# Sums and differences of the up-projection's operands formed on GpSimd instead of VectorE

## The chip, the cores and the metric

The kernel runs on one core of one Trainium2 chip. The metric is device time of one execution in microseconds. A core has five engines with an instruction queue each: TensorE (PE, matmuls), VectorE (DVE), ScalarE (ACT), GpSimd (POOL) and SyncE (SP, which issues most DMAs). Each queue is worked off in order; an instruction that waits holds up everything behind it in its queue. Matmuls read their operands from SBUF and write PSUM.

## The reference

One decoder block over 2048 positions of 1024 channels, in float32:

```
h = rms_norm(x, norm1_g);  z = h @ w_in
y_mix = concat(rg_lru(conv(lru_x)) * gelu(lru_gate),  sc_b * conv(sc_c * sc_x))
x = x + y_mix @ w_out
h = rms_norm(x, norm2_g)
gate, up = split(causal_dwconv(h @ w_up, ffn_conv_w))      # 2 * 3072 columns
x = x + (gelu(gate) * up) @ w_down
return rms_norm(x, final_g)
```

The part that matters is `h @ w_up`: h is 1024 channels by 2048 positions, w_up 1024 by 6144.

## The kernel before

Activations lie with channels on the 128 partitions and positions along the columns. The 2048 positions are handled in two halves of 1024, each half as two blocks of 512 (t0 and t1). Every float32 product is made of three matmuls: each operand is split into a rounded high part and the remainder, the low part, and high x high, high x low and low x high are added. The split (`split`, L196) is one ACT instruction (L197, high) and one DVE instruction (L198, low = source - high).

The three large products (w_out, w_up, w_down) use Strassen's scheme in Winograd's form: seven products of blocks instead of eight, at the price of sums and differences of blocks. For the up-projection the activation's 2 x 2 blocks are a[t0], a[t1] (channels of the upper half) and b[t0], b[t1] (channels of the lower half). `h_prep(half, k, rs)` makes all operands of channel tile k, one of four per half: it loads a and b from DRAM, scales both with the norm (L564), and forms T1 = a0 - a1, T2 = -T1 - b1, T3 = b1 - a1 and T4 = -T2 - b0, of 128 x 512 each. T1 and T2 go into tile hc, T3 over a's second block, T4 into hq. Then a (with T3), b and c are split at 128 x 1024 (hhB/hlB twice, hhT/hlT), and T4 at 128 x 512 (ht).

The program runs through: in-projection and mixers of half 0 and w_out's product ("o"), the same for half 1, up-projection of half 0, w_down's product ("d") of half 0, up-projection of half 1, w_down's product of half 1. A w_out or w_down product is a function `sweeps`: seven sweeps, one for each block product, of three (o) or six (d) steps. A step reads one weight page and one activation page by DMA, splits both (wh/wl and fh/fl), and runs 24 matmuls; the page buffers hold two and a half steps, so the high part of the next-but-one step's activation can be split only when PE is done with a step. Tile names carry sweep and step: fl_o_1_1 is the low part of the activation of sweep 1, step 1 of "o". After a sweep, DVE adds the four PSUM tiles into the results (L785).

The calls of `h_prep` lie beside these products: for half 0 one near the end of half 1's in-projection and three in half 1's "o" product (after its steps 3, 8 and 14, counted from 0); for half 1 four in half 0's "d" product (after steps 4, 12, 25 and 34). Groups are counted from 0 within each half below. The results are used in the up-projection that follows.

The order on PE, SP and GpSimd is that of the program text. ACT and DVE are ordered by a scheduler, from priorities (splits of sweep pages are moved ahead by HW = 90 places) and its own estimate of when inputs are ready. GpSimd has little work: it clears and copies the two or three columns that the convolutions carry from one half to the other (L285, L287, L292), and issues DMAs that add weights (L365).

Of the kernel before, what the change touches and what calls it, by code (L numbers as in the profile page):

```python
# [9 lines left out]
AF = mybir.ActivationFunctionType  # L10
ALU = mybir.AluOpType
# [57 lines left out]
def block_kernel(  # L69
# [11 lines left out]
    nc = tc.nc  # L81
# [35 lines left out]
    def col(o):  # L117
        return g1[:, o : o + 1] if o < KC else prm[:, o - KC : o - KC + 1]
# [4 lines left out]
    def act(name):  # L123
        return page(name, "act", 28)
# [4 lines left out]
    def tmp(name):  # L129
        return page(name, "tmp", 7)  # L130

    def big(name, side):
        return ub.tile([P, T + 3], F32, name=name, tag="ab"[side], bufs=2)
# [10 lines left out]
    def flat(t):  # L144
        return t.rearrange("p a b -> p (a b)")

    def r32(ap):
        return ap.bitcast(F32R)

    def blk(b):  # L150
        return slice(b * NB, (b + 1) * NB)
# [44 lines left out]
    def split(hi, lo, src):  # L196
        nc.scalar.activation(r32(hi), src, AF.Copy)  # L197
        nc.vector.tensor_tensor(r32(lo), src, hi, ALU.subtract)  # L198
# [360 lines left out]
    def h_prep(half, k, rs):  # L559
        a = big(f"ha{half}_{k}", 0)[:, :T]  # L560
        b = big(f"hb{half}_{k}", 0)[:, :T]
        for t, kk in ((a, k), (b, k + 4)):
            nc.sync.dma_start(t, x2_d[half][kk // 2][kk % 2])
            nc.vector.scalar_tensor_tensor(t, t, col(O_G2 + kk), rs, ALU.mult, ALU.mult)  # L564
        c = flat(tmp(f"hc{half}_{k}"))
        q = flat(tmp(f"hq{half}_{k}"))[:, :NB]
        t0, t1 = blk(0), blk(1)
        nc.vector.tensor_tensor(c[:, t0], a[:, t0], a[:, t1], ALU.subtract)
        nc.vector.scalar_tensor_tensor(c[:, t1], c[:, t0], -1.0, b[:, t1], ALU.mult, ALU.subtract)
        nc.vector.tensor_tensor(a[:, t1], b[:, t1], a[:, t1], ALU.subtract)  # L570
        nc.vector.scalar_tensor_tensor(q, c[:, t1], -1.0, b[:, t0], ALU.mult, ALU.subtract)
        out = {}
        for t, names in ((a, ("B11", "T3")), (b, ("B21", "B22")), (c, ("T1", "T2"))):
            hi, lo = act(f"hh{names[0]}{half}_{k}"), act(f"hl{names[0]}{half}_{k}")
            split(flat(hi), flat(lo), t)
            for i, n in enumerate(names):
                out[n] = (hi[:, i, :], lo[:, i, :])
        t4 = act(f"ht{half}_{k}")
        split(t4[:, 0, :], t4[:, 1, :], q)
        out["T4"] = (t4[:, 0, :], t4[:, 1, :])  # L580
        return out

# [281 lines left out]
    def beside_mixers(n):  # L864
        mean0(n)
        if n == NOUT - 2:
            hs[0].append(h_prep(0, 0, rs2[0][0]))
# [10 lines left out]
    def h_beside(half, at):  # L878
        def beside(s):
            if s in at:  # L880
                hs[half].append(h_prep(half, len(hs[half]), rs2[half][0]))

        return beside
# [172 lines left out]
```

## Time and profile before

| What | us |
|---|---|
| median of 3 runs | 2283.89 (2283.12 to 2284.76) |
| the profiled execution's own time | 2283.66 |
| its span, first to last instruction | 2281.9 |
| PE (matmul) busy | 2265.3 (99%) |
| DVE busy | 1723.0 (76%) |
| ACT busy | 1133.6 (50%) |
| POOL busy | 153.3 (7%) |
| mean granted TensorE clock | 0.998 of full speed |

Rows of a timeline read: start, duration (us), engine, line, operation, output<-inputs, shape, count, and in brackets the idle time of the engine before it and what ended it. Rows of groups read: line, engine, operation, tiles, shape, count, busy us, mean ns of one, idle before. Rows of waits read: who waited for whom, then us in total, times, longest. Buffer numbers are left out of names there: fl_o stands for all low parts of "o". A stretch's row (windows) reads: us, then busy us (instruction count) of PE, PEld (TensorE's weight loads), DVE, ACT and POOL, granted clock, share of DMA time, GB/s.

### The profile page before, as it was taken

The page shows a single profiled execution, that of the slowest core. Times are in us where ns is not written, and L with a number is a line of the kernel's source. Part 1 is how long each engine was busy: PE and PEld are TensorE (multiplying, and loading weights), DVE is VectorE, ACT ScalarE, POOL GpSimd, SP SyncE. Part 2 cuts the span into 40 slices and gives each one's busy share as a digit, 9 for nine tenths or more (in the row PEclk, how much of TensorE's full clock was granted, in tenths as well). Part 3 has the DMA queues.
Part 4 walks back from the last instruction along what each step waited for, and adds up shares of the span by engine and source line. Part 5 has one row for each costly group of instructions (what it writes and reads, how often), then busy time and mean ns, then how long its engine had stood idle before and what let it go on. Part 6 is the DMA issues. An engine that isn't in the chain of part 4 may idle for free.

```text
span 2281.9 us, 26199 instructions
## 1 busy us (share of the span) xinstructions
PE 2265.3 (99%) x9982; PEld 1873.6 (82%) x9982; DVE 1723.0 (76%) x1912; ACT 1133.6 (50%) x1247; POOL 153.3 (7%) x232
## 2 busy tenths in 40 slices
PE   9999999999999999999999999999999999999997
PEld 7888888888888878888888888888888888888886
DVE  8765668767657798888888887587888888876556
ACT  6554625554557255544444454354544444444343
POOL 0010000011100000111111100000100000000000
PEclk9999999999999999999999999999999999999999
DMA  7553248778654586233232357676223232359755
GB/s 260 147 125 103 70 162 290 266 195 216 185 135 138 180 280 216 76 104 114 93 115 93 116 188 268 216 243 209 70 97 116 93 116 93 116 182 321 259 193 175
DMA packets 146447, 378.30 MB, mean 166 GB/s; under 512 B 14160, under 2 KB 17872, under 8 KB 145744
## 3 DMA queue, kind: packets, MB, share of 16 engines
q1 hardware_dynamic: 136384, 357.74, 45.4%
q0 software_dynamic: 9792, 18.88, 5.3%
q8 instruction: 78, 1.28, 0.2%
q14 instruction: 49, 0.40, 0.1%
q10 hardware_dynamic: 144, 0.00, 0.0%
HBM read 289.53 MB, written 124.78 MB: 182 GB/s over the span
## 4 chain that ended last, share of the span: by engine, by line
PE 98%; DVE 1%; DMA 0%; issue 0%; ACT 0%; SPq 0%; DVEq 0%
PE zin_b L240 27%; PE zx L628 23%; PE dx L748 11%; PE zc L628 11%; PE dy L748 9%; PE za L628 6%; PE ox L748 6%; PE oy L748 4%; PE zr_b L240 1%; PE zi_b L240 1%; DVE x2r L929 0%; DMA x<-in_xT 0%; DVE fl_o L198 0%; PE ms_b L272 0%; PE ms_a L272 0%
## 5 line engine op out<-in xcount | busy, mean ns | idle before, releaser
L240 PE MATMUL zin_b<-xh,wh_in 128*128 128x512 f32 x896 | 276.2, 389 | 1.0 <-ACT xh L413 0.6
L240 PE MATMUL zin_b<-xl,wh_in 128*128 128x512 f32 x896 | 276.1, 389 | 0.1
L240 PE MATMUL zin_b<-xh,wl_in 128*128 128x512 f32 x896 | 275.9, 389 | 0.0
L240 PEld LDWEIGHTS zin_b<-xh,wh_in 128*128 128x128 f32 x896 | 168.2, 188 | 36.5 <-ACT xh L413 0.9
L240 PEld LDWEIGHTS zin_b<-xl,wh_in 128*128 128x128 f32 x896 | 168.2, 188 | 35.3 <-DVE xl L414 0.5
L240 PEld LDWEIGHTS zin_b<-xh,wl_in 128*128 128x128 f32 x896 | 168.2, 188 | 34.9
L198 DVE TENSOR_TENSOR fl_d<-wrf_d,fh_d 128x1024 fp32r<-128x1024 f32 x84 | 102.8, 1224 | 119.6 <-ACT fh_d L197 117.2
L197 ACT ACTIVATE fh_d<-wrf_d 128x1024 fp32r<-128x1024 f32 x84 | 89.0, 1060 | 201.8 <-PE dx L748 84.3
L198 DVE TENSOR_TENSOR wla_up<-wra_up,wha_up 128x1024 fp32r<-128x1024 f32 x48 | 58.8, 1226 | 140.7 <-ACT wha_up L197 140.6
L748 PE MATMUL dx<-fh_d,wh_d 128*128 128x512 f32 x384 | 149.4, 389 | 0.0
L748 PE MATMUL dx<-fl_d,wh_d 128*128 128x512 f32 x384 | 149.4, 389 | 0.0
L748 PE MATMUL dx<-fh_d,wl_d 128*128 128x512 f32 x384 | 149.4, 389 | 0.0
L628 PE MATMUL zc<-hhB,whd_up 128*128 128x512 f32 x384 | 126.0, 389 | 0.0
L301 DVE SCALAR_TENSOR_TENSOR cu<-un,prm,cu 128x1024 f32<-128x1024 f32 x96 | 122.6, 1277 | 4.3 <-ACT cu L297 4.3
L301 DVE SCALAR_TENSOR_TENSOR cg<-ug,prm,cg 128x1024 f32<-128x1024 f32 x96 | 122.7, 1278 | 0.4
L639 ACT ACTIVATE ug<-zx 128x512 f32<-128x512 f32 x96 | 57.6, 600 | 126.0 <-PE zx L628 126.0
L197 ACT ACTIVATE wh_in<-wr_in 128x1024 fp32r<-128x1024 f32 x53 | 55.7, 1055 | 129.1 <-PE zin_b L240 87.4
L628 PE MATMUL zx<-ht,whc_up 128*128 128x512 f32 x384 | 118.2, 389 | 0.0
L198 DVE TENSOR_TENSOR wl_d<-wrw_d,wh_d 128x1024 fp32r<-128x1024 f32 x84 | 102.4, 1219 | 12.7 <-ACT wh_d L197 11.4
L748 PE MATMUL dy<-fh_d,wh_d 128*128 128x512 f32 x288 | 112.0, 389 | 0.0
L748 PE MATMUL dy<-fl_d,wh_d 128*128 128x512 f32 x288 | 112.0, 389 | 0.0
L748 PE MATMUL dy<-fh_d,wl_d 128*128 128x512 f32 x288 | 112.0, 389 | 0.0
(265 smaller groups left out, 5556.6 us busy)
## 6 DMA issues: line engine op xcount, KB each, us to landing
wr_in<-in_w_in SPq DMA_DIRECT2D x53, 512.0 KB, 6.8
wra_up<-in_w_up SPq DMA_DIRECT2D x48, 512.0 KB, 4.6
wrb_up<-in_w_up SPq DMA_DIRECT2D x48, 512.0 KB, 5.2
f_d_T<-cg SPq DMA_DIRECT2D x96, 256.0 KB, 2.5
wrw_d<-sd_d_S SPq DMA_DIRECT2D x48, 512.0 KB, 4.5
wrf_d<-f_d_T SPq DMA_DIRECT2D x48, 512.0 KB, 3.9
f_d_B<-cu SPq DMA_DIRECT2D x72, 256.0 KB, 2.4
wrw_d<-in_w_down SPq DMA_DIRECT2D x36, 512.0 KB, 4.6
```

What stands on the lines that cost most here:

```text
L197: nc.scalar.activation(r32(hi), src, AF.Copy)
L198: nc.vector.tensor_tensor(r32(lo), src, hi, ALU.subtract)
L240: nc.tensor.matmul(ps[t], r32(a), r32(b[:, blk(t)]), start=(first and i == 0), stop=(last and i == 2))
L301: nc.vector.scalar_tensor_tensor(dst, src[:, k : k + T], col(o_w + k), dst, ALU.mult, ALU.add)
L628: nc.tensor.matmul(ps, r32(p[:, s]), r32(self.hs[k][x][o]), start=f and i == 0, stop=l and i == 2, skip_group_check=True,)
L639: nc.scalar.activation(dst, self.x, AF.Copy)
L748: nc.tensor.matmul(ps[m], r32(p), r32(x[:, k, :]), start=first and i == 0 and n == 0, stop=(last or not on_x) and i == ni - 1 and n == 2, ...
```

## The change

In `h_prep` the four sums and differences move from DVE to GpSimd. GpSimd forms them with plain additions and subtractions, so five are needed: q = a1 - a0, T1 = a0 - a1, T2 = q - b1, T3 = b1 - a1, and q = T2 + b0, which is -T4. The sign of T4 is put right in its split: ACT copies q with scale -1, and DVE forms -q - high in one instruction. All other lines are the same.

```diff
-        nc.vector.tensor_tensor(c[:, t0], a[:, t0], a[:, t1], ALU.subtract)
-        nc.vector.scalar_tensor_tensor(c[:, t1], c[:, t0], -1.0, b[:, t1], ALU.mult, ALU.subtract)
-        nc.vector.tensor_tensor(a[:, t1], b[:, t1], a[:, t1], ALU.subtract)
-        nc.vector.scalar_tensor_tensor(q, c[:, t1], -1.0, b[:, t0], ALU.mult, ALU.subtract)
+        nc.gpsimd.tensor_tensor(q, a[:, t1], a[:, t0], ALU.subtract)
+        nc.gpsimd.tensor_tensor(c[:, t0], a[:, t0], a[:, t1], ALU.subtract)
+        nc.gpsimd.tensor_tensor(c[:, t1], q, b[:, t1], ALU.subtract)
+        nc.gpsimd.tensor_tensor(a[:, t1], b[:, t1], a[:, t1], ALU.subtract)
+        nc.gpsimd.tensor_tensor(q, c[:, t1], b[:, t0], ALU.add)
         out = {}
         for t, names in ((a, ("B11", "T3")), (b, ("B21", "B22")), (c, ("T1", "T2"))):
...
         t4 = act(f"ht{half}_{k}")
-        split(t4[:, 0, :], t4[:, 1, :], q)
+        nc.scalar.activation(r32(t4[:, 0, :]), q, AF.Copy, scale=-1.0)
+        nc.vector.scalar_tensor_tensor(r32(t4[:, 1, :]), q, -1.0, t4[:, 0, :], ALU.mult, ALU.subtract)
```

The scheduler then orders ACT and DVE anew. In the changed kernel the lines of the five sums are L568 to L572, and of T4's split L580 and L581. The first place is group 1 of half 0, in the "o" product of half 1. DVE before:

```order
L564 SCALAR_TENSOR_TENSOR hb_1_5939<-hb_1_5939,prm,ss_b_2593 128x1024
L568 TENSOR_TENSOR hc_1_5944<-ha_1_5938 128x512
L198 TENSOR_TENSOR wl_o_1_1_5970<-wrw_o_1_1_5965,wh_o_1_1_5969 128x1024
L569 SCALAR_TENSOR_TENSOR hc_1_5944<-hc_1_5944,hb_1_5939 128x512
L198 TENSOR_TENSOR fl_o_1_1_5974<-wrf_o_1_1_5967,fh_o_1_1_5973 128x1024
L570 TENSOR_TENSOR ha_1_5938<-hb_1_5939,ha_1_5938 128x512
L571 SCALAR_TENSOR_TENSOR hq_1_5945<-hc_1_5944,hb_1_5939 128x512
L198 TENSOR_TENSOR hlB_1_5951<-ha_1_5938,hhB_1_5950 128x1024
```

DVE in the changed kernel, at the same place:

```order
L564 SCALAR_TENSOR_TENSOR hb_1_5940<-hb_1_5940,prm,ss_b_2593 128x1024
L198 TENSOR_TENSOR wl_o_1_1_5972<-wrw_o_1_1_5967,wh_o_1_1_5971 128x1024
L198 TENSOR_TENSOR hlB_1_5953<-ha_1_5939,hhB_1_5952 128x1024
L198 TENSOR_TENSOR fl_o_1_1_5976<-wrf_o_1_1_5969,fh_o_1_1_5975 128x1024
L198 TENSOR_TENSOR hlB_1_5957<-hb_1_5940,hhB_1_5956 128x1024
L198 TENSOR_TENSOR hlT_1_5961<-hc_1_5945,hhT_1_5960 128x1024
L198 TENSOR_TENSOR wl_o_1_2_6010<-wrw_o_1_2_6005,wh_o_1_2_6009 128x1024
L581 SCALAR_TENSOR_TENSOR ht_1_5964<-hq_1_5946,ht_1_5964 128x512
L198 TENSOR_TENSOR fl_o_1_2_6014<-wrf_o_1_2_6007,fh_o_1_2_6013 128x1024
```

The four sums are gone, and the split of a (hlB_1<-ha_1) now stands ahead of fl_o_1_1 instead of behind it. On ACT the split hhB_1<-ha_1 likewise now stands ahead of fh_o_1_1; it stood behind it.

The second place is group 0 of half 1, in the "d" product of half 0, on DVE. Before, from the split of the page of step 4 on:

```order
L198 TENSOR_TENSOR fl_d_0_4_10216<-wrf_d_0_4_10209,fh_d_0_4_10215 128x1024
L198 TENSOR_TENSOR wl_d_0_5_10280<-wrw_d_0_5_10270,wh_d_0_5_10279 128x1024
L569 SCALAR_TENSOR_TENSOR hc_0_10249<-hc_0_10249,hb_0_10244 128x512
L570 TENSOR_TENSOR ha_0_10243<-hb_0_10244,ha_0_10243 128x512
L571 SCALAR_TENSOR_TENSOR hq_0_10250<-hc_0_10249,hb_0_10244 128x512
L198 TENSOR_TENSOR hlB_0_10256<-ha_0_10243,hhB_0_10255 128x1024
L198 TENSOR_TENSOR fl_d_0_5_10284<-wrf_d_0_5_10272,fh_d_0_5_10283 128x1024
```

In the changed kernel:

```order
L198 TENSOR_TENSOR fl_d_0_4_10220<-wrf_d_0_4_10213,fh_d_0_4_10219 128x1024
L198 TENSOR_TENSOR wl_d_0_5_10285<-wrw_d_0_5_10275,wh_d_0_5_10284 128x1024
L198 TENSOR_TENSOR hlB_0_10261<-ha_0_10247,hhB_0_10260 128x1024
L198 TENSOR_TENSOR hlB_0_10265<-hb_0_10248,hhB_0_10264 128x1024
L198 TENSOR_TENSOR hlT_0_10269<-hc_0_10253,hhT_0_10268 128x1024
L198 TENSOR_TENSOR fl_d_0_5_10289<-wrf_d_0_5_10277,fh_d_0_5_10288 128x1024
```

Before, one split of h_prep stood between the page of step 4 and fl_d_0_5; now three do, and ACT's three (hhB, hhB, hhT) stand ahead of fh_d_0_5 in the same way.

GpSimd's queue takes the five sums where the program text has them; the first group, in the changed kernel:

```order
L365 DMA sd_d_S_3_246<-sd_d_S_3_234 256x512
L568 ISA
L568 TENSOR_TENSOR hq_0_5610<-ha_0_5603 128x512
L569 TENSOR_TENSOR hc_0_5609<-ha_0_5603 128x512
L570 TENSOR_TENSOR hc_0_5609<-hq_0_5610,hb_0_5604 128x512
L571 TENSOR_TENSOR ha_0_5603<-hb_0_5604,ha_0_5603 128x512
L572 TENSOR_TENSOR hq_0_5610<-hc_0_5609,hb_0_5604 128x512
L365 DMA sd_d_S_4_247<-sd_d_S_4_235 256x512
L287 COPY pr_3_5691<-p_halo 128x2
L365 DMA sd_d_S_5_248<-sd_d_S_5_236 256x512
```

The DMAs of L365 add weights of the down-projection; they and the halo copy of pr_3 followed one another directly before.

## The prediction

> **What bounds the kernel now.** I read the page's busy times first, then the waits of PE (TensorE), then the chain that ended last, and only then the stretch around the edited function.
>
> ```profile
> PE 2265.3 (99%) x9982; PEld 1873.6 (82%) x9982; DVE 1723.0 (76%) x1912; ACT 1133.6 (50%) x1247; POOL 153.3 (7%) x232
> PE oy L748 <- DVE fl_o L198: 1.5, 2, 0.9
> PE warm L796 <- POOL eps L97: 1.0, 1, 1.0
> PE zin_b L240 <- ACT xh L413: 0.6, 1, 0.6
> PE zin_b L240 <- ACT wh_in L197: 0.4, 1, 0.4
> ```
>
> PE is busy 99% of the span, and these four lines are all the waiting it does: 3.5 us, of which 2.0 lie at the start. So relieving VectorE (DVE) can win at most 1.5 us, 0.07%. A measurement of this kernel cannot tell less than about 0.2% (4.6 us) from no change. The change can matter only by making PE wait, and the question is whether it does. The chain gives the times at which PE begins its stretches:
>
> ```profile
> 776.92 15.65 PE ox L748 x69
> 828.04 16.32 PE oy L748 x72
> 860.68 16.32 PE oy L748 x72
> 1351.18 32.64 PE dx L748 x144
> 1416.46 32.64 PE dx L748 x144
> 1481.74 32.64 PE dx L748 x144
> 1514.38 32.64 PE dy L748 x144
> ```
>
> 72 matmuls are three steps of a sweep, so a step lasts 16.32/3 = 5.44 us and a matmul 0.23. Each step needs a weight pair and an activation pair, split into high (ACT) and low (DVE). The second matmul of a step reads the low activation part, fl, so fl is due 0.23 us after its step starts. The sum below is about those due times, since h_prep's work stands in the same two in-order queues as the splits.
>
> **The change, removals first.** Four DVE instructions of a group go, and five GpSimd instructions come. A group's place shows here (DVE, group 1 of the first half), with ACT's rows behind it:
>
> ```profile
> 793.21 1.28 DVE L564 SCALAR_TENSOR_TENSOR ha<-ha,prm,ss_b 128x1024 f32<-128x1024 f32 x1
> 795.00 1.28 DVE L564 SCALAR_TENSOR_TENSOR hb<-hb,prm,ss_b 128x1024 f32<-128x1024 f32 x1
> 796.20 0.69 DVE L568 TENSOR_TENSOR hc<-ha 128x512 f32<-128x512 f32 x1
> 796.80 1.22 DVE L198 TENSOR_TENSOR wl_o<-wrw_o,wh_o 128x1024 fp32r<-128x1024 f32 x1
> 798.53 1.22 DVE L198 TENSOR_TENSOR fl_o<-wrf_o,fh_o 128x1024 fp32r<-128x1024 f32 x1
> 802.62 1.22 DVE L198 TENSOR_TENSOR wl_o<-wrw_o,wh_o 128x1024 fp32r<-128x1024 f32 x1
> 803.76 1.22 DVE L198 TENSOR_TENSOR hlB<-hb,hhB 128x1024 fp32r<-128x1024 f32 x1
> 804.89 1.22 DVE L198 TENSOR_TENSOR fl_o<-wrf_o,fh_o 128x1024 fp32r<-128x1024 f32 x1
> ...
> 800.39 1.06 ACT L197 ACTIVATE hhB<-ha 128x1024 fp32r<-128x1024 f32 x1 [6.27 <-DVE ha L570]
> 801.35 1.05 ACT L197 ACTIVATE wh_o<-wrw_o 128x1024 fp32r<-128x1024 f32 x1
> 802.30 1.04 ACT L197 ACTIVATE hhB<-hb 128x1024 fp32r<-128x1024 f32 x1
> ```
>
> In a full queue DVE starts a 512-column instruction every 0.60 us (796.20 to 796.80), a 1024-column split every 1.14 (802.62 to 803.76) and a scaling of L564 every 1.20 (795.00 to 796.20); ACT starts a split every 0.95. So DVE sheds 4 x 0.60 = 2.4 us a group, 19 us in eight groups, none of it on PE's path except in the 1.5 us above. The two rewritten instructions of T4 keep engine, size and place: nothing.
>
> **What one GpSimd sum costs.** The profile has no such instruction; these are the nearest rows.
>
> ```profile
> L93 POOL MEMSET ones<- 128x128 f32 x1 | 0.2, 204 | 0.3 <-POOLq L1043 0.3
> L97 POOL MEMSET eps<- 128x1 f32 x1 | 0.1, 98 | 0.0
> L285 POOL MEMSET ug<- 128x2 f32 x24 | 2.4, 100 | 219.1 <-DVE hlB L198 146.5 <-DVE cg L301 72.6
> L292 POOL COPY u_halo<-ug 128x2 f32<-128x2 f32 x24 | 39.0, 1624 | 215.0 <-DVE ug L643 215.0
> 1110.11 1.78 POOL L292 COPY u_halo<-ug 128x2 f32<-128x2 f32 x1 [8.99 <-DVE ug L643]
> 1109.97 1.27 DVE L301 SCALAR_TENSOR_TENSOR cu<-un,prm,cu 128x1024 f32<-128x1024 f32 x1
> 1111.16 0.68 DVE L604 TENSOR_TENSOR wra_up<-wra_up,wrb_up 128x512 f32<-128x512 f32 x1
> ```
>
> 127 more columns of a memset cost 204 - 98 = 106 ns, 0.83 ns a column: 0.43 us for 512, 0.10 fixed. One pass is thus 0.53 us, the lower end; two reads one after the other 0.95; two reads and a write 1.38, the upper end. I take 1.17, halfway between the last two, because two operands must be read and only how far the write overlaps is open. [...]
>
> **Whether the two engines share a port.** A memset of two columns, which reads nothing, takes 0.10 us; a copy of two columns takes 1.62 on average. The copy at 1110.11 ends at 1111.89, right after the two DVE instructions with two SBUF operands beside it end (1111.16 + 0.68 = 1111.84). GpSimd's read waited them out. A GpSimd sum should therefore run only while no such DVE instruction runs: every two-operand DVE instruction between the scaling of a and the first split that waits for GpSimd delays the chain by its whole length. Which of the two goes first does not matter to the sum. [...]
>
> **What moves, and who waits.** ACT's split of a (hhB<-ha) needs T3, the fourth sum, and in the new order it and DVE's hlB stand ahead of the fl split that PE needs next. Lateness = (end of a's scaling + DVE work C in between + 4 x 1.17 = 4.68 + tail) - due time. The other places:
>
> ```profile
> 819.62 1.28 DVE L564 SCALAR_TENSOR_TENSOR ha<-ha,prm,ss_b 128x1024 f32<-128x1024 f32 x1
> 847.54 1.28 DVE L564 SCALAR_TENSOR_TENSOR ha<-ha,prm,ss_b 128x1024 f32<-128x1024 f32 x1
> 1365.55 1.28 DVE L564 SCALAR_TENSOR_TENSOR ha<-ha,prm,ss_b 128x1024 f32<-128x1024 f32 x1
> 1408.77 1.28 DVE L564 SCALAR_TENSOR_TENSOR ha<-ha,prm,ss_b 128x1024 f32<-128x1024 f32 x1
> 1486.72 1.28 DVE L564 SCALAR_TENSOR_TENSOR hb<-hb,prm,ss_b 128x1024 f32<-128x1024 f32 x1
> 1528.49 1.28 DVE L564 SCALAR_TENSOR_TENSOR ha<-ha,prm,ss_b 128x1024 f32<-128x1024 f32 x1
> 755.13 1.23 DVE L198 TENSOR_TENSOR hlB<-ha,hhB 128x1024 fp32r<-128x1024 f32 x1 [0.53 <-ACT hhB L197]
> ```
>
> First half, group 0: its splits run around 755, and the first split queued behind them is for the step at 776.92 + 5.44 = 782.4. Over 20 us of cover: 0. Were that cover gone, it would cost what group 1 does. On GpSimd this group stands ahead of two sums of down-projection weights by DMA, first read from 1351.18 on, and of a halo copy whose reader waits for PE's last in-projection, which ends at 776.92; an ISA instruction ahead of the first sum lies under the same cover.
> Group 1: 793.21 + 1.28 = 794.5. C = 1.20 (hb) + 1.14 (wl) = 2.3. Tail = hhB 1.06, hlB 1.14, fl 1.22 = 3.4. fl lands at 804.9; due 776.92 + 4 x 5.44 + 0.23 = 798.9. Late 6.0. PE waited 1.5 here before, and the next fl (five DVE instructions, 5.2 us, behind) now just makes its step, so 4.5 net.
> Group 2: 820.9 + 2.3 + 4.7 + 3.4 = 831.3; due 828.04 + 0.23. Late 3.1.
> Group 3: 848.8, C = wl, an add, hb, fl, wl = 5.2, tail with a second hlB 4.6: 863.3; due 860.9. Late 2.4.
> Second half, group 0: 1366.8, C = hb, fl, wl = 3.5, tail = hhB, hlB, hlB, hlT, fl = 5.7: 1380.7; due 1351.18 + 5 x 5.44 + 0.23 = 1378.6. Late 2.1.
> Group 1: 1410.05 + 3.5 + 4.7 + tail 5.8 (hhB, hlB, four residual adds of 0.60, fl) = 1424.0; due 1416.46 + 5.44 + 0.23 = 1422.1. Late 1.9.
> Group 2: a is scaled early, so from the end of hb, 1488.0: C = 2.9, two sums 2.3, tail 5.7: 1498.9; due 1481.74 + 16.32 + 0.23 = 1498.3. Late 0.6.
> Group 3: 1529.8 + 3.5 + 4.7 + 5.7 = 1543.6; due 1514.38 + 27.20 + 0.23 = 1541.8. Late 1.8.
> The later splits are paced by PE, so lateness adds up: 4.5 + 3.1 + 2.4 + 2.1 + 1.9 + 0.6 + 1.8 = 16.4 us. Against the profiled execution, 2283.66 (span 2281.9 and 1.8 around it), that is 2300.1; the median of the runs, 2283.89, lies 0.2 higher, so 2300.3, 0.7% slower.
>
> A wait of 6 us could also touch PE's clock. The row of the stretch with the old waits (PE busy 7.50 of 9.00 us) grants 1.00:
>
> ```profile
> 798.00:807.00 9.00, 7.50 (x33) 5.52 (x32) 8.47 (x10) 6.61 (x8) 0.00 (x0) 1.00 0.55 176
> ```
>
> So I add nothing for it. [...]
>
> **Bounds.** 0.1 us per sum moves six groups by 0.4 us and one by 0.2. At 1.38: 16.4 + 6 x 0.84 + 0.42 = 21.9, 2305.8. At 0.95: 10.7, 2294.6. At 0.53 only group 1 (1.9) and group 2 (0.5) stay late: 2286.3.
>
> **Rivals.** No shared port, so not slower by what can be measured: GpSimd runs beside DVE, C is 0 except that the third sum waits for hb. Group 1 then costs 6.0 - 2.3 - 1.5 = 2.2 and group 2 0.7; the others have 1.4 us or more to spare (second half, group 0: 1377.2 against 1378.6). 2286.8, no change. The point that decides is C: below about 1.4 us per group the second half hides everything. Against it speak the 1.62 us copies.
> Longer sums: each sum waits for its predecessor's semaphore and loses the port to a DVE instruction that slips in, so that one takes 1.6 us in effect. 16.4 + 6 x 1.72 + 0.86 = 27.6: 2311.5. For it: the copy at 1110.11 let a second DVE instruction pass. Against it: DVE soon stands still at hlB.
> Short sums, 0.53 to 0.95 with a shared port: 2286 to 2295. Against it: two operands through one port in one pass.
> Relief of DVE: the old 1.5 us vanish and nothing else appears, 2282.4, still no change; it needs ACT and DVE not to be held at hhB and hlB, which the new order contradicts.
>
> **How the numbers follow.** Forecast 0.70, longer sums 0.09, short sums 0.07, no shared port 0.12, relief 0.02. 0.2% slower begins at 2288.5: forecast, longer and half of short give 0.82, cut to 0.80 for what I have not seen; same 0.18; faster 0.02. The range runs from 2286, which takes in the lower bound and the unshared port, to 2310, past the upper bound of 2305.8; about 0.15 is left outside.
>
> **What would show it.** PE's waits should name fl_o and fl_d (or their ACT halves) with some 18 us in about seven places, the longest near 6 us around 799; the five sums should take 1.0 to 1.4 us when DVE is still and up to 2.6 when it runs; hhB<-ha should wait for GpSimd's L571. If fl splits are not late in the second half, the port or the size of a sum is wrong; if a group's lateness differs from its neighbours by more than 1 us from the above, it is C. Were PE's waits unchanged at 3.5 us, the whole argument would fall.

## The result and the profile after

| | before | after |
|---|---|---|
| median of 4 runs each, us | 2284.26 (2283.12 to 2284.76) | 2310.19 (2309.24 to 2311.63) |
| span of the profiled execution, us | 2281.9 | 2308.7 |
| mean granted TensorE clock | 0.998 | 0.993 |

The changed kernel is slower: 1.0116 times the time of before, 95% interval 1.0104 to 1.0128, or 25.9 us. 16.4 had been forecast, and the time lies 0.2 us beyond the upper end of the range.

The page's busy times come first, then PE's waits:

```profile
PE 2278.1 (99%) x9982; PEld 1880.3 (81%) x9982; DVE 1717.7 (74%) x1880; ACT 1132.3 (49%) x1247; POOL 227.1 (10%) x272
```

```profile
PE oy L750 <- ACT fh_o L197: 7.3, 3, 4.9
PE dx L750 <- DVE fl_d L198: 4.6, 3, 1.9
PE oy L750 <- DVE fl_o L198: 2.7, 3, 1.1
PE dy L750 <- DVE fl_d L198: 1.3, 1, 1.3
PE dx L750 <- ACT fh_d L197: 0.5, 1, 0.5
PE dy L750 <- ACT fh_d L197: 0.2, 1, 0.2
```

With the start of the program, PE waits 18.2 us instead of 3.5: 14.7 more, at fl and fh of both products, as forecast. But PE is also busy 12.8 us longer (2278.1 against 2265.3) with the same 9982 matmuls. The two add up to 27.5 us, the span's 26.8 to within 0.7. Nothing in the prediction's sum made a matmul longer.

First the part that was forecast. Group 1 of the first half after the change, on DVE, ACT and GpSimd in turn:

```profile
793.08 1.28 DVE L564 SCALAR_TENSOR_TENSOR ha<-ha,prm,ss_b 128x1024 f32<-128x1024 f32 x1
794.28 0.68 DVE L787 TENSOR_TENSOR xr<-xr,ox 128x512 f32<-128x512 f32 x1
794.87 1.95 DVE L564 SCALAR_TENSOR_TENSOR hb<-hb,prm,ss_b 128x1024 f32<-128x1024 f32 x1
796.74 2.31 DVE L198 TENSOR_TENSOR wl_o<-wrw_o,wh_o 128x1024 fp32r<-128x1024 f32 x1
802.51 1.23 DVE L198 TENSOR_TENSOR hlB<-ha,hhB 128x1024 fp32r<-128x1024 f32 x1 [3.46 <-ACT hhB L197]
803.65 1.22 DVE L198 TENSOR_TENSOR fl_o<-wrf_o,fh_o 128x1024 fp32r<-128x1024 f32 x1
...
801.42 1.06 ACT L197 ACTIVATE hhB<-ha 128x1024 fp32r<-128x1024 f32 x1 [11.88 <-POOL ha L571]
...
794.44 1.30 POOL L568 TENSOR_TENSOR hq<-ha 128x512 f32<-128x512 f32 x1 [54.71 <-DVE ha L564]
795.69 2.27 POOL L569 TENSOR_TENSOR hc<-ha 128x512 f32<-128x512 f32 x1
797.93 2.24 POOL L570 TENSOR_TENSOR hc<-hq,hb 128x512 f32<-128x512 f32 x1
800.13 1.26 POOL L571 TENSOR_TENSOR ha<-hb,ha 128x512 f32<-128x512 f32 x1
801.35 1.26 POOL L572 TENSOR_TENSOR hq<-hc,hb 128x512 f32<-128x512 f32 x1
```

A sum beside an idle DVE takes 1.26 us (800.13). Beside a busy DVE it is recorded with 2.27, and DVE's rows grow as well: the split wl_o from 1.22 to 2.31. The two take turns, and these turns are all that "port" stands for below; what makes them no row shows. hb's scaling ends at 796.82, the sum issued at 795.69 then runs until 797.96, and wl_o until 799.05. ACT's split of a waits for the fourth sum (T3), DVE stands still for 3.46 us at hlB, and fl_o lands at 803.65 + 1.22 = 804.87. The forecast was 804.9.

Now the part that was not. Away from the program's start and end, TensorE's granted clock was at half for 3.41, 6.83 or 10.24 us at a time in these runs: it changed only at the ends of stretches of 3.41 us (the stretches at full clock between those at half were 27.31, 34.13, 563.20 and 122.88 us in the changed kernel, 8, 10, 165 and 36 times 3.41), called clock steps here to tell them from the steps of a sweep. These rows of windows are cut along the clock steps (us, then busy us with instruction counts of PE, PEld, DVE, ACT and POOL, granted clock, DMA share, GB/s):

```profile
797.16:800.57 3.41, 1.40 (x7) 0.82 (x5) 1.89 (x1) 0.00 (x0) 3.41 (x3) 1.00 0.15 25
800.57:803.98 3.41, 0.50 (x1) 0.29 (x1) 1.47 (x2) 2.56 (x3) 2.04 (x2) 0.50 0.33 129
803.98:807.40 3.42, 2.77 (x7) 1.99 (x7) 3.42 (x4) 3.42 (x5) 0.00 (x0) 0.50 0.42 140
807.40:810.81 3.41, 3.41 (x10) 2.64 (x9) 3.41 (x4) 1.28 (x2) 0.00 (x0) 0.50 0.43 145
834.70:838.11 3.41, 0.85 (x4) 0.28 (x2) 2.51 (x3) 3.41 (x4) 1.02 (x1) 1.00 0.00 0
838.11:841.52 3.41, 3.41 (x8) 2.68 (x9) 3.41 (x5) 3.14 (x4) 0.00 (x0) 0.50 0.61 189
1394.48:1397.89 3.41, 1.93 (x7) 1.37 (x8) 3.41 (x4) 3.41 (x5) 0.00 (x0) 1.00 0.16 38
1397.89:1401.30 3.41, 3.41 (x17) 2.80 (x16) 3.41 (x5) 0.07 (x1) 0.00 (x0) 1.00 1.03 346
1438.85:1442.27 3.42, 1.50 (x8) 0.93 (x6) 3.42 (x6) 3.42 (x5) 0.00 (x0) 1.00 0.00 0
1442.27:1445.68 3.41, 3.41 (x8) 2.76 (x9) 3.41 (x6) 1.33 (x2) 0.00 (x0) 0.50 0.48 154
1565.15:1568.56 3.41, 1.84 (x8) 1.08 (x7) 3.41 (x5) 3.41 (x5) 0.00 (x0) 1.00 0.08 11
1568.56:1571.97 3.41, 3.41 (x10) 2.63 (x9) 2.87 (x3) 0.41 (x1) 0.00 (x0) 0.50 0.94 305
```

Where PE was busy for 1.84 us or less of such a step, the next one ran at half clock although PE had work again: 10 matmuls from 1568.56, against 17 after 1397.89, where PE had been busy 1.93. Seven clock steps ran at half, three of them in one piece after group 1. Counted from the start of one matmul to the next (0.227 us at full clock), between 700 and 1650 us, the rows at half clock lose 9.5 us and the waits 20.0; before it was 0 and 2.05. How a wait inside a row at half clock is shared out moves some tenths between the two.

### The profile page after: what moved, and what is told of

It reads as the page before. It is cut to its first block, busy times and chain, and to the rows that moved or that the text cites. A ratio compares the mean times of both kernels' runs of the same rounds, so it can differ in the third digit from the quotient of the medians.

```text
span 2308.7 us, 26248 instructions
## 1 busy us (share of the span) xinstructions
PE 2278.1 (99%) x9982; PEld 1880.3 (81%) x9982; DVE 1717.7 (74%) x1880; ACT 1132.3 (49%) x1247; POOL 227.1 (10%) x272
## 3 DMA queue, kind: packets, MB, share of 16 engines
q8 instruction: 78, 1.28, 0.2%
## 4 chain that ended last, share of the span: by engine, by line
PE 90%; DVE 3%; issue 3%; POOL 1%; ACT 1%; DMA 1%; SPq 0%; DVEq 0%; POOLq 0%; ACTq 0%
PE zin_b L240 24%; PE zx L630 23%; PE zc L630 11%; PE dx L750 9%; PE dy L750 7%; PE za L630 6%; PE oy L750 4%; PE ox L750 4%; PE zr_b L240 1%; PE zi_b L240 1%; POOL hc L570 1%; POOL ha L571 0%; DVE fl_d L198 0%; ACT hhB L197 0%; DMA wrw_o<-in_w_out 0%
```

## The experiments

Each is an edit of the changed kernel, if nothing else is said, and is compared with runs of the kernel before on the same chip (medians of 2283.2 to 2283.4 us). For each run "waits" and "half clock" are counted as just described.

| Kernel | median us | against before, us (ratio, 95%) | waits | half clock |
|---|---|---|---|---|
| before | 2284.3 | | 2.05 | 0 |
| after | 2310.2 | +25.9 (1.0104 to 1.0128) | 20.0 | 9.5 |
| second half only | 2295.0 | +11.7 (1.0033 to 1.0067) | 10.0 | 3.2 |
| filled waits | 2305.4 | +22.1 (1.0078 to 1.0108) | 10.1 | 1.6 |
| filled, same order | 2302.0 | +18.6 (1.0067 to 1.0098) | 7.6 | 0 |
| T3 on DVE | 2299.5 | +16.2 (1.0054 to 1.0084) | 15.7 | 1.7 |
| splits later | 2299.8 | +16.5 (1.0054 to 1.0084) | 12.9 | 5.8 |
| later, last group early | 2293.4 | +10.0 (1.0026 to 1.0060) | 7.7 | 3.4 |
| second half only, later | 2283.3 | -0.1 (0.9991 to 1.0009) | 2.07 | 0 |
| T4 alone | 2284.2 | +0.8 (0.9994 to 1.0013) | 2.07 | 0 |
| first half's sums on DVE, later | 2287.6 | +4.4 (1.0007 to 1.0026) | 4.5 | 1.7 |

In each row without fills, waits and half clock less the 2.05 of before give the difference to within 1.6 us, so these two leave little else to explain.

**Theories.** For each of the two parts, two causes stood against each other. For the clock: it is a cost of its own, or it falls into time that PE would have waited anyway. For the waits: the splits of a group stand in ACT's and DVE's queues, waiting for GpSimd, ahead of splits that PE needs (order), or GpSimd takes the port from DVE (port).

**One product alone.** Half 0's groups are back on DVE, T4's split in the form that goes with it; half 1's, in the "d" product, stay on GpSimd.

```diff
+        if half == 1:
             nc.gpsimd.tensor_tensor(q, a[:, t1], a[:, t0], ALU.subtract)
...
+        else:
+            nc.vector.tensor_tensor(c[:, t0], a[:, t0], a[:, t1], ALU.subtract)
```

> The five sums stay on GpSimd only for the four groups of the second half, which are prepared in the d product of half 0; the first half's groups are back on VectorE. Theory (each product pays for its own late splits, waits plus the clock windows that these cause): the changed kernel lost 15.9 us in the o product and 11.8 us in the d product, so 2284.3 + 11.8 = 2296 us, made of 8.3 us of waits on fl_d and fh_d and one or two windows of 3.41 us at half clock; with none of these windows 2292.6, with two 2296, with three 2299.5. The stretch from 770 to 900 us should read as before, with 1.5 us of waiting and a granted clock of 1.00. Rival (the d product is late only because the o product passed its lateness on): no more than 2286.

Measured: 2295.0. The waits of this kernel:

```profile
PE dx L759 <- DVE fl_d L198: 4.5, 3, 1.9
PE oy L759 <- DVE fl_o L198: 1.5, 2, 0.9
```

fl_o is as before the change, fl_d as after it (4.5 against 4.6): "d" pays for its own groups, and its loss is not handed on from "o". Two clock steps at half, 3.2 us, came with it.

**Filling the waits.** Matmuls of zeros (fills) are put where PE waits, so that it is busy without doing anything useful.

```diff
+                for _ in range(FILL.get((name, half, s, i2), 0)):
+                    nc.tensor.matmul(
+                        ps[0][:, :P], ones, ones_r.bitcast(F32), start=first and i2 == 0, stop=False, skip_group_check=True
+                    )
```

with `ones` set to zero meanwhile. The second kernel differs in one number:

```diff
-    ("o", 1, 5, 0): 8,
+    ("o", 1, 5, 0): 2,
```

> The changed kernel with short matmuls of zeros put into seven of PE's waits, ahead of the steps whose low activation part is late: 20, 10 and 8 in the o product, 7, 7, 5 and 7 in the d product, each 128x128 and an estimated 0.2 us; they add zero to sums that are being accumulated, and nothing else changes. PE does about 13 us more work, in time that it waited. Theory (9.5 us of the loss is PE at half clock after waits that made a window of 3.41 us idle by 2 us or more): the windows at 800, 838, 875, 1442 and 1568 us go, the granted clock is 1.00 from 700 to 1650 us, and the time falls from 2310.2 to some 2301 (2299 to 2303 if one fill is a little too long or one window stays). Rival (the whole loss is the waits, and the half clock costs nothing because PE would have waited in that time anyway): 2310 or slower by what the fills overshoot.

> As the kernel with the filled waits, but with 2 instead of 8 matmuls of zeros ahead of sweep 5's first step in the o product; with 8 the order of VectorE's queue had changed there (the split hlT of the last group came to stand ahead of a low split that PE needs), which made a new wait of 2.03 us at 882.6 and a window at half clock. With 2 the order is that of the changed kernel. Theory (the clock term): no half-clock window is left, or one, and the time is 2300 to 2302.5 us, some 9 us under the changed kernel although PE executes 58 more matmuls. Rival (the half clock costs little of its own, and the fills win by something else): it stays at 2305 or above.

Measured: 2305.4 and 2302.0. In the first, half the expected gain came: it has a new wait and a clock step at half. The cause is in its VectorE rows: hlT had moved ahead of fl_o and waited there for a store out of the page that it writes.

```profile
882.48 1.23 DVE L207 TENSOR_TENSOR hlT<-hc,hhT 128x1024 fp32r<-128x1024 f32 x1 [2.57 <-DMA x_d<-xr]
883.62 1.22 DVE L207 TENSOR_TENSOR fl_o<-wrf_o,fh_o 128x1024 fp32r<-128x1024 f32 x1
```

The second has the changed kernel's order, and the expected time. The stretch from 797 to 811 us in the changed kernel, and then in this one:

```profile
797.00:811.00 14.00, 8.43 (x23) 6.00 (x23) 10.54 (x9) 7.26 (x8) 5.61 (x4) 0.63 0.34 111
```

```profile
797.00:811.00 14.00, 12.58 (x75) 10.81 (x74) 10.39 (x9) 8.32 (x9) 5.34 (x4) 1.00 0.33 114
```

The clock is 1.00 here and in every other place where it had fallen. Eight fills, which the trace records as two matmuls each, take 1.70 us from the start of the first to that of the matmul behind the last (869.23 to 870.93 in the first of the two kernels), 0.21 each; by this estimate 58 take some 12.3, and with 7.6 us of waits that is 19.9, near the 20.0 of the changed kernel. The splits were as late as there: fl_o of group 1 lands at 804.59, 11.8 us after a's scaling starts, as in the changed kernel. So PE had 58 fills more to do, and the time fell by 8.2 us, or by 7.3 if each kernel is taken against its own runs of before. The half clock is a cost of its own.

**T3 back on DVE.** The split of a then waits for no GpSimd sum directly.

```diff
-        nc.gpsimd.tensor_tensor(a[:, t1], b[:, t1], a[:, t1], ALU.subtract)
+        nc.vector.tensor_tensor(a[:, t1], b[:, t1], a[:, t1], ALU.subtract)
```

> Four of the five sums stay on GpSimd; only the one that the split of a waits for, T3 = b1 - a1, is back on VectorE. It must still wait for GpSimd's two sums that read a1. Theory (what costs is the chain ahead of the split of a): two sums of 1.2 to 2.3 us leave the chain and one VectorE sum of 0.6 us comes in, so each low split lands 2 to 3.5 us earlier. In the first group of the o product that leaves some 3 us of lateness, 1.5 of it already there before; the six other places were late by 0.8 to 2.5 us and end on time or just late. No window reaches 2 us of idle time save perhaps the first. 2286 to 2290 us. Rival (each sum on GpSimd costs its share, by the port that it takes from VectorE): four fifths of 25.9 us stay, 2305.

Measured: 2299.5, between the two expectations, so neither holds. VectorE's rows of group 1:

```profile
795.15 1.94 DVE L564 SCALAR_TENSOR_TENSOR hb<-hb,prm,ss_b 128x1024 f32<-128x1024 f32 x1
798.27 1.75 DVE L571 TENSOR_TENSOR ha<-hb,ha 128x512 f32<-128x512 f32 x1 [1.18 <-POOL hc L569]
799.95 2.29 DVE L198 TENSOR_TENSOR wl_o<-wrw_o,wh_o 128x1024 fp32r<-128x1024 f32 x1
803.30 1.21 DVE L198 TENSOR_TENSOR fl_o<-wrf_o,fh_o 128x1024 fp32r<-128x1024 f32 x1
```

T3 overwrites a1, which GpSimd's first two sums read, so DVE now stands still at T3, and wl_o, which had run during GpSimd's chain (796.74), stands behind it (799.95). fl_o lands at 804.51, 0.36 us earlier only. What the expectation left out is the queue of the instruction that was moved back.

**The splits made later.** All sums stay on GpSimd; the splits come three steps after the scaling. `gate` is the high activation part of that later step.

```diff
+            g = gate[:, 0, 0:1].bitcast(F32)
+            nc.gpsimd.tensor_tensor(mark, g, g, ALU.subtract)
+            for t in (a, c, q):
+                nc.gpsimd.tensor_tensor(t[:, 0:1], t[:, 0:1], mark, ALU.add)
```

> All five sums stay on GpSimd, and the splits of a group are made three sweep steps (16 us) later than its scaling: ahead of them GpSimd adds a zero, taken from the high activation part of that later step, to one column of each of the three sources, so that neither the split of a nor that of c or q can be put into ScalarE's and VectorE's queues before. This adds four one-column GpSimd instructions a group. Theory (the loss is that hhB and hlB stood in the two queues, waiting for GpSimd, ahead of the splits that PE needs next): the waits of PE on fl_o, fh_o, fl_d and fh_d fall from 16.6 to at most 3 us, the clock stays at 1.00, and the time is 2282.5 to 2287. Rival (the loss is the port: GpSimd's reads hold up VectorE's splits, and that stays as it is, since the sums run at the same places): 2295 to 2305, with waits on fl at the same seven places.

Measured: 2299.8, far above the theory's range and inside the rival's, but not with the rival's seven waits. Three of the four "d" groups no longer make PE wait at all, which is the order; but three places remain, and one of them, at the fourth "d" group, has a new cause. SyncE's rows there, and DVE's and ACT's:

```profile
1547.99 0.32 SPq L774 DMA_DIRECT2D wrf_d<-f_d_T  x1
1561.68 2.11 SPq L927 DMA_DIRECT2D x2r<-x_d  x2
1563.84 0.46 SPq L774 DMA_DIRECT2D wrw_d<-in_w_down  x1
...
1560.43 1.23 DVE L199 TENSOR_TENSOR hlB<-ha,hhB 128x1024 fp32r<-128x1024 f32 x1 [0.58 <-ACT hhB L198]
...
1568.41 1.06 ACT L198 ACTIVATE wh_d<-wrw_d 128x1024 fp32r<-128x1024 f32 x1 [5.60 <-DMA wrw_d<-in_w_down]
```

SyncE's queue issued nothing for 13.7 us: the residual load x2r takes the page of ha, which the late split gives back at 1560.43 + 1.23 = 1561.66, and the weight loads stood behind it. The next kernel scales this group three steps earlier (after step 31 instead of 34):

```diff
-    h_beside(1, (4, 12, 25, 34)),
+    h_beside(1, (4, 12, 25, 31)),
```

> As the kernel whose splits come three steps later, but the last group of the second half is scaled and summed three steps earlier, so that its splits end where they ended before. In that kernel this group's pages were held three steps longer, the residual load that takes one of them stood first in SyncE's queue until 1561.7 us, and the weight loads behind it made PE wait 5.1 us and clock two windows at half. Theory: these 5.1 us and about 3 us of clock go, everything else stays, 2299.8 - 8 = 2291.5 us (2290 to 2293); what is left (9 us of waits and half clock around 800 and 830 us, where GpSimd's sums stretch the low splits from 1.2 to 2.3 us) is the price of the shared port in the crowded product. Rival (the port costs as much in the second half, and was hidden behind this wait): 2295 or more, with new waits on fl_d.

Measured: 2293.4, 0.4 us above the range; all waiting in "d" is gone, and 9 us of waits and half clock remain, all in "o". Next the same with the first half's groups as before the change:

```diff
+        if half == 1:
             nc.gpsimd.tensor_tensor(q, a[:, t1], a[:, t0], ALU.subtract)
...
-            if s - LATER in at:
+                if half == 0:
+                    hs[half].append(held.pop()(None))
+            if half == 1 and s - LATER in at:
```

> The kernel of the run before, with the first half's groups back on VectorE and with their splits where the kernel before had them: twenty sums on GpSimd, all of the second half. Theory (in the d product neither the sums nor the port costs anything once no split waits for GpSimd ahead of a split that PE needs): as the kernel before, 2282.5 to 2285.5 us, with 1.5 us of waits on fl_o and none on fl_d, though VectorE's rows beside the sums still take up to 2.3 us. Rival (the port costs by itself): 2287 or more.

Measured: 2283.3, no change against before. Twenty sums run on GpSimd, and DVE's splits are stretched beside them (GpSimd's rows, then DVE's, in the "d" product):

```profile
1373.25 1.29 POOL L573 TENSOR_TENSOR ha<-hb,ha 128x512 f32<-128x512 f32 x1
1374.50 2.27 POOL L574 TENSOR_TENSOR hq<-hc,hb 128x512 f32<-128x512 f32 x1
...
1373.49 2.13 DVE L199 TENSOR_TENSOR fl_d<-wrf_d,fh_d 128x1024 fp32r<-128x1024 f32 x1 [1.35 <-ACT fh_d L198]
1375.55 2.31 DVE L199 TENSOR_TENSOR wl_d<-wrw_d,wh_d 128x1024 fp32r<-128x1024 f32 x1
```

but there DVE has the slack, and PE doesn't notice. So in "d" the sums and the port cost nothing once the splits that wait for them stand behind those that PE needs: the 11.7 us came through the order. That the port had no part in them is not shown. The changed kernel's first and fourth sum of the same group:

```profile
1382.66 2.27 POOL L568 TENSOR_TENSOR hq<-ha 128x512 f32<-128x512 f32 x1 [12.68 <-DMA wrw_d<-in_w_down]
...
1389.36 1.29 POOL L571 TENSOR_TENSOR ha<-hb,ha 128x512 f32<-128x512 f32 x1
```

The four sums ahead of the split of a take 7.99 us; four at 1.26 would take 5.04. The 2.95 between them is more than the 2.3 us by which this group was late. By this estimate it took both, the order and the port, to make it late, and to take away one of them is enough. The other three "d" groups come out alike: 7.93 and 7.92 us for four sums, late by 2.1 and 2.0, and 5.28 instead of 2.52 for the two sums behind hb in the third, late by 1.6.

**What is left in "o".** The kernel with the last group early and the splits late in both halves, but the first half's sums back on DVE:

```diff
+        if half == 1:
             nc.gpsimd.tensor_tensor(q, a[:, t1], a[:, t0], ALU.subtract)
...
+        else:
+            nc.vector.tensor_tensor(c[:, t0], a[:, t0], a[:, t1], ALU.subtract)
```

> As the kernel with all splits later and the last group early (2293.4 us), but the first half's sums are made on VectorE in the kernel before's form; the splits stay three steps later in both halves and the second half's sums stay on GpSimd. It tells what the 10 us that were left there are made of. Theory (the port: GpSimd's sums stretch VectorE's scaling and low splits around 800 and 831 us): with the sums on VectorE nothing is stretched, each sum costs 0.6 us of VectorE's own time, and the time is 2283 to 2286. Rival (the pile-up: the first group's splits, moved three steps, now stand right ahead of the second group's scaling and push its low splits late, whoever makes the sums): the waits of 5.0 us around 831 us stay and one window at half clock with them, 2288 to 2291.

Measured: 2287.6 (before, in this comparison: 2283.2), between the two expectations. The pile-up is real, though it is in SyncE's queue and not on DVE, where it was expected. At the second group:

```profile
821.08 0.32 SPq L564 DMA_DIRECT2D hb<-x_d  x1
821.46 0.43 SPq L783 DMA_DIRECT2D wrw_o<-in_w_out  x1
...
819.79 1.22 DVE L199 TENSOR_TENSOR hlB<-hb,hhB 128x1024 fp32r<-128x1024 f32 x1
...
825.89 1.06 ACT L198 ACTIVATE wh_o<-wrw_o 128x1024 fp32r<-128x1024 f32 x1 [7.36 <-DMA wrw_o<-in_w_out]
```

The load of the next hb waits for the late split of the last one (it ends at 821.01), and the weights again stand behind it. That is 4.4 us of the 10.0. The other 5.6 (4.8 by the two traces, between the same two matmuls near 780 and 1600 us) come and go with the engine that makes the sums, while the splits stay late: the port. The low split of group 1, first with the sums on GpSimd ("later, last group early"), then with them on DVE:

```profile
800.44 2.28 DVE L199 TENSOR_TENSOR fl_o<-wrf_o,fh_o 128x1024 fp32r<-128x1024 f32 x1
```

```profile
798.53 1.22 DVE L199 TENSOR_TENSOR fl_o<-wrf_o,fh_o 128x1024 fp32r<-128x1024 f32 x1
```

DVE's splits and scalings there stand in the same order in both. From start to start PE waits 2.7 us around 800 us with the sums on GpSimd and 1.1 with them on DVE, and 5.0 and 3.3 around 830; a clock step at half follows the first place in the former alone and the second in both. In the second group DVE's adds of PSUM tiles stand in another order too, so there the port is not the only difference.

**One sum alone.** An edit of the kernel before: T4 on GpSimd, with T4's split in the change's form, the other three on DVE:

```diff
-        nc.vector.scalar_tensor_tensor(q, c[:, t1], -1.0, b[:, t0], ALU.mult, ALU.subtract)
+        nc.gpsimd.tensor_tensor(q, c[:, t1], b[:, t0], ALU.add)
```

> Of the sums only the last one, T4 = c1 + b0, goes to GpSimd, with its negation in the split of q as in the change; T1, T2 and T3 stay on VectorE in the kernel before's form. The split of a doesn't wait for GpSimd, and only the split of q, the last of the group, does. Theory (position in the chain decides, not the number of sums): at most one or two VectorE instructions are held up by 1.1 us beside each sum, which costs 0 to 1.2 us in the first group of the o product, where PE waited before, and nothing elsewhere: 2283.3 to 2285.5. Rival (each sum costs its share of the port, a fifth of 25.9 us): 2288.5.

Measured: 2284.2, no change. A fifth of the loss would have been 5.2 us.

## Why the prediction was too low

Its steps in order:

1. PE bounds the kernel, and relieving DVE is worth nothing: held. The kernels with one sum or twenty on GpSimd and no new waits are not faster than before, by 0.8 and -0.1 us. Less than its 0.2% can be told, though: "first half's sums on DVE, later" is slower by 0.17%, with an interval that leaves out no change.
2. A sum at 1.17 us: 1.26 alone, within its bounds.
3. A shared port: the turns held, and in both directions (a sum 2.27 us beside a busy DVE instead of 1.26, wl_o 2.31 beside a sum instead of 1.22); the prediction had rows for GpSimd's side only.
4. The lateness of each group, with PE's excess from start to start at that place:

| Group | forecast | measured |
|---|---|---|
| first half, 1 | 6.0 | 6.3 |
| first half, 2 | 3.1 | 3.0 |
| first half, 3 | 2.4 | 2.3 |
| second half, 0 | 2.1 | 2.3 |
| second half, 1 | 1.9 | 2.1 |
| second half, 2 | 0.6 | 1.6 |
| second half, 3 | 1.8 | 2.0 |
| sum | 17.9 | 19.6 |

With 0.4 us after the waits this is the 20.0 of above. Net of before's 2.05 it is 18.0, where the prediction had 16.4 net of 1.5. Only one place is off by more than 0.3 us: there hb was scaled 22.7 us later than before while PE's steps had moved by 22.0, and why is not shown. Group 0 of the first half cost nothing, as forecast.

5. "A wait of 6 us could also touch PE's clock ... So I add nothing for it": this is the step that failed. The term was taken as 0 and measured 9.5 us, 7.3 to 8.2 by the fills. The row behind it had PE busy 7.50 of 9.00 us, a waiting of 1.5 us in all; it says nothing of a wait of 5. And 2 us of waiting in one clock step were enough, so that nearly every one of the seven waits was in question, not the one of 6 us alone. 16.4 + 1.6 + 9.5 = 27.5 against a span longer by 26.8.

In a clock step at half in which PE was busy throughout, matmuls started every 0.427 us instead of 0.227 (838.54 to 841.53: seven in 2.99 us). That costs 3.41 x (1 - 0.227/0.427) = 1.6 us of such a step. In the seven at half (the one not shown, from 875.66, busy throughout) PE is busy 20.3 us in all, by the same share 9.5 us of work lost, as counted.

Of the rivals, "longer sums" came nearest in time (2311.5) with the wrong cause: less the 2.3 us of DVE work between them, the four sums of group 1 (794.44 to 801.39) took 1.2 us each in effect, not 1.6, and PE would have waited some 28 us more, not 18. No shared port, short sums and relief of DVE are out by the rows of group 1.

## What to carry to other kernels

An instruction moved to an idle engine is paid for where its reader stands: if the reader waits in an in-order queue ahead of work that the bounding engine needs next, the whole chain is late (in "d" here by 11.7 us), and moving the reader behind that work made the same sums free (-0.1 us), as long as the pages it then holds longer don't block a load queue (SyncE's issued nothing for 13.7 us here). Before an engine at 99% is made to wait, count the waits against its clock: here each clock step of 3.41 us with 2 us or more of waiting was followed by one at half, worth up to another 1.6 us. And where no row covers waits of the size that is forecast, the term belongs into the range, not at zero.

## What the runs showed that was not expected

The clock. Between 700 and 1650 us, over all these runs, 19 clock steps in which PE stood idle for 2.00 us or more (from start to start, less 0.227) were each followed by one at half; no clock step at full clock with 1.76 us or less was, and nothing between was measured. In the changed kernel those at full clock stood idle for 2.99 (from 834.70), 2.29 (872.25), 2.17 (797.16), 2.08 (1438.85) and 2.00 us (1565.15), and 1.76 (1394.48) was not followed by one. One that is itself at half was followed by another with less waiting: after 803.98 PE was busy 2.77 of 3.42 us, and the next was at half again. The clock steps don't start with the wait, so waits of some 2 us cost up to another 1.6 us or nothing here, as they fell into one clock step or across two: the one at 1439 us was followed by one at half, and the two waits around 1394 us (2.27 together, 1.76 of it in one clock step) weren't.

The port. DVE rows with one operand in PSUM were not stretched beside a sum: xr<-xr,ox at 794.28 takes 0.68 us while GpSimd's first sum runs (794.44, 1.30 us), and so does each of the three x2r<-x2r,dy from 1502.70 to 1504.58, beside a sum of 1.29 us (1502.93). The scaling of hb at 794.87, with hb and ss_b both in SBUF, takes 1.95 instead of 1.28. The rows show turns by whole instructions: after this scaling (796.82) the sum issued at 795.69 ends 1.14 us later (797.96), and wl_o another 1.09 later (799.05).
